# Sums of forms run ahead of their high parts, low parts a step behind, in an FFN's last two up-projections

## The chip, the cores and the metric

The kernel runs on one core of a Trainium2 chip. The metric is the time of one execution in device microseconds (us). A profile of one execution tells what each engine did: TensorE (PE, with PEld for its weight loads), VectorE (DVE), ScalarE (ACT), GpSimd (POOL) and SyncE (SP), which issues most of the loads.

## The reference

A trunk of two layers over 512 frames of width 1024. Each layer has an FFN, a mixer (an mLSTM in the first, a gated MLP in the second), a second FFN and a gated embedding, with a LayerNorm after each. The change touches the four FFNs:

```python
def swiglu_ffn(x, w_gu, w_d):          # w_gu 1024 x 5632, w_d 2816 x 1024
    g, u = jnp.split(x @ w_gu, 2, axis=-1)
    return (jax.nn.silu(g) * u) @ w_d
x = layer_norm(DN_ALPHA * x + 0.5 * swiglu_ffn(x, ffn1_wgu[i], ffn1_wd[i]), ln_g[i, 0], ln_b[i, 0])
```

## The kernel before

**Splitting.** Every float32 operand of a matmul is split in two: a high part, which ScalarE makes by a copy (`whi`, `fhi`), and a low part, the operand less the high part, which VectorE makes by a subtraction (`wlo`, `flo`). A product of two operands is three matmuls (`mm3`, L318 to L320). Some low parts (list `by_dma`, product numbers 1, 2 and 4 of each seven) are made without VectorE: ScalarE writes minus the high part, and GpSimd issues a transfer that adds the operand to it (L243, L244).

**Chunks.** The 2816 hidden columns of an FFN are 22 blocks of 128, worked in six chunks (`FFN_CHUNKS`). The first four chunks are projected up plainly (`fps`). The last two, from `UP_FROM` = 4 on, are projected up by seven products in the place of eight, the Winograd form of Strassen's product, for two blocks (a pair) at a time: `up_products`. So an FFN has four pairs, and 28 products up (`ups`), which the text calls p0 to p27; the number within a pair is r = 0 to 6. The weights of a pair lie in two tiles of 1 MB, `g` and `u`, of two quarters each. Its seven operands are, in order, a11, a12, s2, s1, s3, s4, a22; s1 to s4 are sums, which VectorE makes in place in those quarters (`up_forms`; L139, L140 make s1 and s2, L147 makes s3, L151 makes s4). x's own seven operands are made by `UpForms`: most of them by `steps` during chunk 3, the rest in `last`, at the end of chunk 3.

**Down.** The product down of a chunk (`gps`) is done by seven products too, one after every second product up of the next chunk. Its weights are formed by `forms` (`wquarter`, L110 to L116) and its left operands, the hidden values, by `Group.form` (`h`, `fhi`, `flo`). `Group.add` adds a product to the residual `xt`.

**Order.** The order of instructions on each engine is that in which the code is written; each engine works through its own in order, and waits at an instruction whose operands are not there. In `up_products` a step s issues: the product up; the addition of an earlier product down to `xt`; `pair.take`, which for r = 0, 2 and 3 copies the bank out on ScalarE (L977) and else adds it on VectorE (L980, L985) or multiplies the gate in (L994); `W.release`, which gives the weight's buffer back and so forms and splits the operand four products ahead (`fill`); and, every second step, the product down and the next form of `h`. All r = 0, 2, 4 and 6 of a pair accumulate in one bank, so p(r = 4) can't start before the copy of r = 2, and p(r = 2) not before that of r = 0.

Of the kernel before, what the change touches and what calls it, by code (L numbers as in the profile page):

```python
# [17 lines left out]
P = 128  # L18
# [30 lines left out]
class Weights:  # L49
# [4 lines left out]
    def __init__(self, nc, raw_pool, split_pool):  # L54
# [7 lines left out]
        self.ready, self.taken, self.held = deque(), deque(), []  # L62

# [33 lines left out]
    def forms(self, kind, b11, b12, b22, b21):  # L97
# [23 lines left out]
        for _, make in made:  # L121
            self.in_place.add(make)
        return [(kind, js, make) for js, make in made]

    def up_forms(self, g, u):
# [12 lines left out]
        def s2():  # L138
            vec.tensor_add(quarter(u, 0), quarter(u, 0), quarter(u, 1))  # L139
            vec.tensor_sub(quarter(g, 0), quarter(u, 0), quarter(g, 0))  # L140
            return quarter(g, 0), (g,)

        def s1():
            return quarter(u, 0), ()

        def s3():
            vec.tensor_sub(quarter(u, 0), quarter(u, 1), quarter(g, 0))  # L147
# [65 lines left out]
    def fill(self, most=1000, low=None, meanwhile=None):  # L213

        while most and self.next_split < len(self.order):
# [8 lines left out]
            if js is not None:  # L224
                src, used = make()
                shape = list(src.shape)
# [8 lines left out]
            for i in range(parts):  # L235
# [9 lines left out]
                else:  # L245
# [3 lines left out]
            for j in used:  # L249
                self.left[j] -= 1  # L250
            while self.load():
                pass
        return meanwhile

    def take(self):
# [5 lines left out]
        self.kind, tiles = self.ready.popleft()  # L261
        if not self.kind.startswith("rows"):
            self.taken.append(self.kind)
# [24 lines left out]
def hybrid_trunk(ctx: ExitStack, tc, x, p, ln_g, ln_b, ffn1_wgu, ffn1_wd, ffn2_wgu, ffn2_wd,  # L288
# [540 lines left out]
    class Group:  # L829
# [5 lines left out]
        def __init__(self, h, pool, first=False, by_tokens=False):  # L835
# [4 lines left out]
            self.ready, self.banks = deque(), []  # L840
            self.next_form = self.next_product = self.next_add = 0

        def form(self):

            def a(i, j):
                m = self.half
                if self.by_tokens:
                    return self.h[:, 2 * i - 2:2 * i, (j - 1) * 256:j * 256]
                return self.h[:, m * j - m:m * j, (i - 1) * 256:i * 256]
            a11, a12, a21, a22 = a(1, 1), a(1, 2), a(2, 1), a(2, 2)  # L850
# [4 lines left out]
            if r == 2:  # L855
                vec.tensor_add(a21, a21, a22)
                vec.tensor_sub(a11, a21, a11)  # L857
# [5 lines left out]
            split(hi, lo, (a11, a12, a11, a21, a21, a12, a22)[r])  # L863
            self.ready.append((hi, lo))

        def product(self):
            r = self.next_product
            self.next_product += 1
            w, f = W.take(), self.ready.popleft()
# [21 lines left out]
    class UpForms:  # L891


        def __init__(self, pool, late):
# [36 lines left out]
            def last():  # L931
                split(*self.t3, b)
                d = [tmp_tile("x_d").rearrange("p (k t) -> p k t", k=2) for _ in range(2)]
                for i, s in enumerate(halves):
                    joined(d[i], 1, 0, s)
                    vec.tensor_sub(d[i], d[i], c[:, s])
                vec.tensor_sub(f32r(self.t2, late, "wlo"), c, self.t2[0].bitcast(F32))
                hi, lo = f32r(self.t4, pool, "f1"), f32r(self.t4, pool, "f0")
                for i, s in enumerate(halves):
                    split(hi[:, s], lo[:, s], d[i])  # L940

            self.last = last
# [10 lines left out]
    class UpPair:  # L953
# [19 lines left out]
        def take(self, r):  # L973
# [4 lines left out]
            elif r in (1, 5):  # L978
                g = part[r // 5 * 2]
                vec.tensor_add(g, g, bank[1 if r == 1 else 3])  # L980
                sca.activation(g, g, AF.Silu)
                if r == 5:
                    self.gated(1, g, part[3])
# [4 lines left out]
            if r in (1, 5, 6):  # L988
                up_let_go(self.at[{1: 1, 5: 3, 6: 0}[r]])

# [837 lines left out]
```

## Time and profile before

| | |
|---|---|
| time, median of 3 runs (lowest to highest) | 2350.91 us (2349.48 to 2351.85) |
| the profiled execution | 2349.07 us, its span 2347.4 us |
| PE busy in the span | 2234.5 us (95%) |
| DVE busy | 1716.2 us (73%) |
| ACT busy | 1051.8 us (45%) |
| mean granted clock of TensorE | 0.978 |

A row of a timeline has the start and the length in us, the engine, the line, the operation, out<-in, the shapes, and in brackets the idle time before it and what ended that. A row of windows has a stretch and its length, then the busy time of each engine in it (with the number of instructions), the granted clock of TensorE as a share of full speed, and the share of the transfer engines with their GB/s. A row of waits has engine, line and tile, whom it waited for, us in all, times, and the longest.

### The profile page before, as it was taken

What the parts mean: (1) busy time and instruction counts of PE and PEld (TensorE: products, weight loads), DVE (VectorE), ACT (ScalarE), POOL (GpSimd) and SP (SyncE); (2) the same over time, 40 slices, a digit from 0 to 9 for tenths busy, and PEclk for the clock granted to TensorE, in tenths of its full rate; (3) what the DMA queues carried; (4) which work ended last, traced back from release to release, by engine and by line L of the source; (5) the groups of instructions that cost most, each with busy time, mean ns of one, the idle gap of its engine ahead of it and who ended that gap; (6) DMA issues with size and microseconds to landing.
All of it is one profiled execution on the core that took longest, in us unless ns stands there. A gap on an engine that the chain in (4) does not pass through costs nothing.

```text
span 2347.4 us, 29405 instructions
## 1 busy us (share of the span) xinstructions
PE 2234.5 (95%) x11669; PEld 1922.8 (82%) x11669; DVE 1716.2 (73%) x2468; ACT 1051.8 (45%) x1476; POOL 145.0 (6%) x183
## 2 busy tenths in 40 slices
PE   9999889999999999988899998979999999998898
PEld 8887878888888888877788887878888888887877
DVE  5668677786776676777786768776788767686787
ACT  4334445564646533444444334445345443345442
POOL 1000000111101000000000000000001000000000
PEclk9999889999999999999999999999999999998999
DMA  6324434556846533344433324433438633345341
GB/s 202 111 82 129 117 81 135 126 134 135 163 108 142 153 108 99 108 99 126 126 122 94 124 71 122 126 95 121 142 83 153 170 99 108 99 117 138 87 133 65
DMA packets 213233, 278.91 MB, mean 119 GB/s; under 512 B 6580, under 2 KB 161332, under 8 KB 213096
## 3 DMA queue, kind: packets, MB, share of 16 engines
q1 hardware_dynamic: 168080, 211.83, 27.9%
q0 software_dynamic: 38400, 50.52, 13.8%
q10 hardware_dynamic: 6616, 14.69, 1.8%
q8 instruction: 92, 1.51, 0.3%
q14 instruction: 45, 0.37, 0.1%
HBM read 224.58 MB, written 2.11 MB: 97 GB/s over the span
## 4 chain that ended last, share of the span: by engine, by line
PE 76%; DVE 12%; ACT 6%; issue 4%; DMA 0%; ACTq 0%; POOL 0%; DVEq 0%; POOLq 0%
PE fps L318 8%; PE fps L320 7%; PE fps L319 7%; PE gps L318 5%; PE gps L319 5%; PE gps L320 5%; DVE wlo L246 3%; ACT whi L237 3%; PE ups L318 2%; PE dps L318 2%; PE dps L320 2%; PE dps L319 2%; PE ups L319 2%; PE ups L320 2%; DVE xt L692 2%
## 5 line engine op out<-in xcount | busy, mean ns | idle before, releaser
L237 ACT ACTIVATE whi<-wraw 128x1024 fp32r<-128x1024 f32 (+1 forms) x388 | 400.4, 1048 | 209.1 <-DVE wraw L147 47.9
L246 DVE TENSOR_TENSOR wlo<-wraw,whi 128x1024 fp32r<-128x1024 f32 (+1 forms) x292 | 350.0, 1217 | 81.3 <-ACT whi L237 80.5
L246 DVE TENSOR_TENSOR wlo<-wquarter,whi 128x1024 fp32r<-128x1024 f32 (+1 forms) x140 | 156.3, 1117 | 232.2 <-ACT whi L237 232.2
L318 PE MATMUL fps<-xh,whi 128*128 128x512 f32 x800 | 311.4, 389 | 0.0
L319 PE MATMUL fps<-xl,whi 128*128 128x512 f32 x800 | 311.2, 389 | 0.0
L320 PE MATMUL fps<-xh,wlo 128*128 128x512 f32 x800 | 311.2, 389 | 0.0
L237 ACT ACTIVATE whi<-wquarter 128x1024 fp32r<-128x1024 f32 (+1 forms) x140 | 135.8, 970 | 268.9 <-PE gps L320 103.7
L318 PE MATMUL gps<-whi,fhi 128*128 128x512 f32 x644 | 253.0, 393 | 0.0
L319 PE MATMUL gps<-wlo,fhi 128*128 128x512 f32 x644 | 252.1, 392 | 0.0
L320 PE MATMUL gps<-whi,flo 128*128 128x512 f32 x644 | 251.3, 390 | 0.0
L318 PE MATMUL ups<-xh,whi 128*128 128x256 f32 x512 | 158.9, 310 | 70.4 <-ACT us L977 70.4
L244 POOL DMA_DIRECT2D wlo<-wraw x96 | 100.6, 1048 | 1576.1 <-ACT wlo L243 1493.4
L692 DVE TENSOR_TENSOR xt<-xt,gps 128x512 f32<-128x512 f32 x302 | 193.0, 679 | 0.7 <-PE gps L320 0.7
L320 PEld LDWEIGHTS fps<-xh,wlo 128*128 128x128 f32 x800 | 150.2, 188 | 31.4
L319 PEld LDWEIGHTS fps<-xl,whi 128*128 128x128 f32 x800 | 150.2, 188 | 31.0
L318 PEld LDWEIGHTS fps<-xh,whi 128*128 128x128 f32 x800 | 150.2, 188 | 30.9
L318 PEld LDWEIGHTS ups<-xh,whi 128*128 128x128 f32 x512 | 110.1, 215 | 76.3 <-ACT us L977 75.4
L323 ACT ACTIVATE fhi<-h 128x512 fp32r<-128x512 f32 (+1 forms) x140 | 81.4, 581 | 194.4 <-DVE h L857 53.0
L319 PE MATMUL ups<-xl,whi 128*128 128x256 f32 x512 | 156.1, 305 | 0.0
L320 PE MATMUL ups<-xh,wlo 128*128 128x256 f32 x512 | 155.9, 304 | 0.0
L320 PEld LDWEIGHTS gps<-whi,flo 128*128 128x128 f32 x644 | 121.3, 188 | 26.6
L318 PEld LDWEIGHTS gps<-whi,fhi 128*128 128x128 f32 x644 | 121.8, 189 | 23.9
(357 smaller groups left out, 4964.7 us busy)
## 6 DMA issues: line engine op xcount, KB each, us to landing
wraw<-in_ffn_wgu_dram SPq DMA_DIRECT2D x79, 1024.0 KB, 6.4
wlo<-wraw POOLq DMA_DIRECT2D x96, 512.0 KB, 5.2
wquarter<-in_ffn_wd_dram SPq DMA_DIRECT2D x64, 512.0 KB, 3.8
wraw<-in_ml_w_in_dram SPq DMA_DIRECT2D x24, 1024.0 KB, 5.6
wraw<-in_gm_w_in_dram SPq DMA_DIRECT2D x15, 1024.0 KB, 5.7
wraw<-in_ffn_wgu_dram SPq DMA_DIRECT2D x17, 512.0 KB, 5.0
wraw<-in_ffn_wd_dram SPq DMA_DIRECT2D x8, 1024.0 KB, 4.8
wraw<-in_ml_w_out_dram SPq DMA_DIRECT2D x8, 1024.0 KB, 5.2
```

Source lines behind the costliest of these rows:

```text
L237: self.nc.scalar.activation(hi[:, s], src[:, s], AF.Copy)
L244: self.nc.gpsimd.dma_start(lo[:, s], src[:, s], accum_op=OP.add)
L246: self.nc.vector.tensor_sub(lo[:, s], src[:, s], hi[:, s].bitcast(F32))
L318: mm(ps, st[0], mv[0], start=start, stop=False, skip_group_check=more)
L319: mm(ps, st[0], mv[1], start=False, stop=False, skip_group_check=more)
L320: mm(ps, st[1], mv[0], start=False, stop=stop, skip_group_check=more)
L323: sca.activation(hi, src, AF.Copy)
L692: vec.tensor_add(dst, dst, ps)
```

## The change

In `up_products`, and there alone, three things are apart that were together. `form_ahead` makes the sums of the next three operands in the order as soon as what they overwrite has been split. A low part of VectorE's is not made behind its high part but put on a list, which the next step empties (`lows`, `finish_form`). And x's last operands, made in one go at the end of chunk 3 before, are made at steps 0, 2, 3 and 4 of chunk 4 (`formed.last`). With them: s3 is made in g's first quarter (where s2 was) after s4 in g's second, silu is issued behind the next split (`gate`), and the gate of r = 5 a step later. In `Group`, for all who use it, one subtraction moves from form 5 to form 4, and form 4 has another tile.

ScalarE between the copy of r = 0 and that of r = 3 in the first pair, before. `us` is the value copied out of a bank `ups`; `whi<-wraw` is the high part of an operand up, `whi<-wquarter` that of a weight down. What an instruction waits for stands behind it:

```order
L977 ACTIVATE us_1793<-ups_1768 128x512 [waits PE_49]
L237 ACTIVATE whi_1796<-wraw_1527 128x1024 [waits DVE_49]
L243 ACTIVATE wlo_1797<-wraw_1527 128x1024
L981 ACTIVATE us_1793<-us_1793 128x512 [waits DVE_49]
L237 ACTIVATE whi_1829<-wraw_1470 128x1024 [waits DVE_49,PE_49,Activation_49]
L237 ACTIVATE whi_1851<-wquarter_1145 128x1024 [waits DVE_49,PE_49,Activation_49]
L323 ACTIVATE fhi_1857<-h_1296 128x512 [waits DVE_49,Activation_49]
L977 ACTIVATE us_1887<-ups_1768 128x512 [waits PE_49]
L237 ACTIVATE whi_1889<-wraw_1527 128x1024
L977 ACTIVATE us_1920<-ups_1895 128x512 [waits PE_49,Activation_49]
```

And of the changed kernel:

```order
L1045 ACTIVATE us_1779<-ups_1754 128x512 [waits PE_49]
L358 ACTIVATE xh_87<-x_wlo_1299 128x4x256
L242 ACTIVATE whi_1787<-wraw_1472 128x1024 [waits DVE_49]
L248 ACTIVATE wlo_1788<-wraw_1472 128x1024
L242 ACTIVATE whi_1820<-wraw_1472 128x1024 [waits PE_49,Activation_49]
L1059 ACTIVATE us_1779<-us_1779 128x512 [waits DVE_49]
L242 ACTIVATE whi_1838<-wquarter_1145 128x1024 [waits PE_49,Activation_49]
L905 ACTIVATE fhi_1843<-h_1296 128x512 [waits DVE_49,Activation_49]
L1045 ACTIVATE us_1872<-ups_1754 128x512 [waits PE_49]
L242 ACTIVATE whi_1881<-wraw_1530 128x1024
L1045 ACTIVATE us_1911<-ups_1886 128x512 [waits PE_49]
```

The copies stand where they stood; two of the three high parts between the first two copies no longer wait for VectorE, and x's high part (L358) has come behind the first copy.

VectorE from the sum s2 of the second pair on, before (`wraw` are the quarters up, `wquarter` the weights down):

```order
L139 TENSOR_TENSOR wraw_1833<-wraw_1833 128x1024 [waits DMAHW2_49]
L140 TENSOR_TENSOR wraw_1588<-wraw_1833,wraw_1588 128x1024 [waits DVE_49]
L246 TENSOR_TENSOR wlo_2031<-wquarter_1407,whi_2030 128x1024 [waits Activation_49]
L859 TENSOR_TENSOR h_1296<-h_1296 128x2x256
L324 TENSOR_TENSOR flo_2038<-h_1296,fhi_2037 128x512 [waits PE_49,Activation_49]
L692 TENSOR_TENSOR xt_86<-xt_86,gps_1835 128x512
L692 TENSOR_TENSOR xt_86<-xt_86,gps_1836 128x512
L994 SCALAR_TENSOR_TENSOR h_1767<-us_1793,ups_1768 128x2x256 [waits PE_49]
L246 TENSOR_TENSOR wlo_2069<-wraw_1833,whi_2068 128x1024 [waits Activation_49]
L147 TENSOR_TENSOR wraw_1833<-wraw_1833,wraw_1588 128x1024 [waits DVE_49]
```

And of the changed kernel (DMAHW is a load of SP's, DMASW a transfer of GpSimd's):

```order
L141 TENSOR_TENSOR wraw_1876<-wraw_1876 128x1024 [waits DMAHW2_49,DMASW6_49]
L142 TENSOR_TENSOR wraw_1590<-wraw_1876,wraw_1590 128x1024 [waits DVE_49]
L1048 TENSOR_TENSOR us_1872<-us_1872,ups_1886 128x512 [waits PE_49]
L149 TENSOR_TENSOR wraw_1590<-wraw_1590 128x1024 [waits DMASW7_49,DVE_49,Activation_49]
L150 TENSOR_TENSOR wraw_1590<-wraw_1876,wraw_1590 128x1024 [waits DMASW0_49,DVE_49,Activation_49]
L727 TENSOR_TENSOR xt_86<-xt_86,gps_1824 128x512 [waits PE_49]
L727 TENSOR_TENSOR xt_86<-xt_86,gps_1825 128x512 [waits PE_49]
L1064 SCALAR_TENSOR_TENSOR h_1753<-us_1872,us_1911 128x2x256 [waits Activation_49]
L1064 SCALAR_TENSOR_TENSOR h_1753<-us_1779,ups_1754 128x2x256 [waits PE_49]
L908 TENSOR_TENSOR flo_2037<-h_1296,fhi_2036 128x512 [waits Activation_49]
L257 TENSOR_TENSOR wlo_2034<-wquarter_1409,whi_2033 128x1024
```

s3 (L149, L150; L147 before) has come from the tenth place to the fourth and fifth, and waits for two transfers of GpSimd's, those of a12's and s2's low parts. DMASW7 is the one and DMASW0 the other.

VectorE where x's last operands are made, in the first pair, before (`x_d` and `t_f` are x's fourth sum and its parts, which p6 reads):

```order
L324 TENSOR_TENSOR flo_1748<-h_1296,fhi_1747 128x512 [waits Activation_49]
L324 TENSOR_TENSOR xl_88<-x_wlo_1299,xh_87 128x4x256 [waits Activation_49]
L905 TENSOR_TENSOR x_d_1753<-xh_87,xl_88 128x512
L936 TENSOR_TENSOR x_d_1753<-x_d_1753,x_f0_1300 128x512 [waits DVE_49]
L905 TENSOR_TENSOR x_d_1754<-xh_87,xl_88 128x512
L936 TENSOR_TENSOR x_d_1754<-x_d_1754,x_f0_1300 128x512 [waits DVE_49]
L937 TENSOR_TENSOR t_wlo_1759<-x_f0_1300,t_whi_1651 128x1024
L324 TENSOR_TENSOR t_f0_1762<-x_d_1753,t_f1_1761 128x512 [waits DVE_49,Activation_49]
L324 TENSOR_TENSOR t_f0_1762<-x_d_1754,t_f1_1761 128x512 [waits Activation_49]
L147 TENSOR_TENSOR wraw_1527<-wraw_1527,wraw_1470 128x1024
```

And the end of the same work in the changed kernel, between steps 3 and 4:

```order
L257 TENSOR_TENSOR wlo_1882<-wraw_1530,whi_1881 128x1024 [waits PE_49,Activation_49]
L1002 TENSOR_TENSOR x_d_1302<-x_d_1302,x_f0_1300 128x512
L1002 TENSOR_TENSOR x_d_1303<-x_d_1303,x_f0_1300 128x512
L727 TENSOR_TENSOR xt_86<-xt_86,gps_1924 128x512 [waits PE_49]
L727 TENSOR_TENSOR xt_86<-xt_86,gps_1925 128x512 [waits PE_49]
L1050 TENSOR_TENSOR us_1911<-us_1911,ups_1754 128x512 [waits PE_49,Activation_49]
L908 TENSOR_TENSOR flo_1942<-h_1296,fhi_1941 128x512 [waits Activation_49]
L892 TENSOR_TENSOR h_1296<-h_1296 128x2x256
L893 TENSOR_TENSOR h_1296<-h_1296 128x2x256 [waits DVE_49]
L257 TENSOR_TENSOR wlo_1922<-wraw_1590,whi_1921 128x1024 [waits DMAHW1_49]
L257 TENSOR_TENSOR wlo_1939<-wquarter_1145,whi_1938 128x1024
L1008 TENSOR_TENSOR t_f0_1978<-x_d_1302,t_f1_1917 128x512
```

The low part of x's fourth sum, ahead of all sums and low parts of the pair before, now stands behind those of four steps. The order of TensorE, GpSimd and SP is as it was. The diff, cut to its core:

```diff
@@ up_forms
         def s2():
             vec.tensor_add(quarter(u, 0), quarter(u, 0), quarter(u, 1))
             vec.tensor_sub(quarter(g, 0), quarter(u, 0), quarter(g, 0))
+            return quarter(g, 0), ()
+        def s1():
+            return quarter(u, 0), (u,)
+        def s3():
+            vec.tensor_sub(quarter(g, 1), quarter(g, 1), quarter(g, 0))
+            vec.tensor_sub(quarter(g, 0), quarter(u, 1), quarter(g, 0))
             return quarter(g, 0), (g,)
-        def s1():
-            return quarter(u, 0), ()
-        def s3():
-            vec.tensor_sub(quarter(u, 0), quarter(u, 1), quarter(g, 0))
-            return quarter(u, 0), (u,)
         def s4():
-            vec.tensor_sub(quarter(g, 1), quarter(g, 1), quarter(g, 0))
             return quarter(g, 1), (g,)
...
+        self.after.update({s2: (a11,), s3: (a12, s2)})
@@ fill
-                src, used = make()
+                while any(m not in self.formed for m in self.after.get(make, ())):
+                    self.lows(1)
+                src, used = self.made.pop(make, None) or make()
...
-                else:
+                elif not self.apart:
                     self.nc.vector.tensor_sub(lo[:, s], src[:, s], hi[:, s].bitcast(F32))
...
-            for j in used:
-                self.left[j] -= 1
-            while self.load():
-                pass
+            def done(make=make, used=used, src=src, hi=hi, lo=lo, late=self.apart and make not in self.by_dma):
+                if late:
+                    self.nc.vector.tensor_sub(lo, src, hi.bitcast(F32))
+                self.formed.add(make)
+                for j in used:
+                    self.left[j] -= 1
+                while self.load():
+                    pass
+            if self.apart and make not in self.by_dma:
+                self.pending.append((lo, done))
+            else:
+                done()
+    def lows(self, most=100):
+        for _ in range(min(most, len(self.pending))):
+            self.pending.popleft()[1]()
+    def form_ahead(self, n):
+        for kind, js, make in self.order[self.next_split:self.next_split + n]:
+            if js is None or make in self.made or make not in self.in_place:
+                continue
+            if any(m not in self.formed for m in self.after.get(make, ())):
+                continue
...
+            self.made[make] = make()
@@ Group
+        def sums(self, r):
...
+            elif r == 4:
+                vec.tensor_sub(a12, a12, a11)
+                vec.tensor_sub(a11, a22, a11)
...
-            elif r == 4:
-                vec.tensor_sub(a21, a22, a11)
-            elif r == 5:
-                vec.tensor_sub(a12, a12, a11)
...
+            def low():
+                vec.tensor_sub(lo, src, hi.bitcast(F32))
+                self.low = None
+                if r in (1, 3) and apart:
+                    self.sums(r + 1)
+                    self.summed.add(r + 1)
@@ UpForms
-            def last():
-                split(*self.t3, b)
-                d = [tmp_tile("x_d").rearrange("p (k t) -> p k t", k=2) for _ in range(2)]
...
+            d = [tmp.tile([P, 2, 256], F32, name="x_d", tag="pad", bufs=3) for _ in range(2)]
...
+            self.last = {0: t3_t2, 2: x21, 3: t4, 4: t4_low}
@@ up_products, step s
+                    if r == 6:
+                        pair.gated(1, pair.part[2], pair.part[3])
                     pair.take(r)
+                    group.finish_form()
+                    W.lows()
+                    if c == UP_FROM and s in formed.last:
+                        formed.last[s]()
                     W.release()
+                    pair.gate(r)
+                    W.form_ahead(3)
                     if s % 2:
                         group.product()
                         W.release(kind="rows")
-                        group.form()
+                        group.form(True)
```

More of the change, by code (lines that the diff above doesn't have):

```diff
@@ L122, in forms @@
             self.in_place.add(make)
+        self.after.update({t2: (made[0][1],), t1: (made[1][1], t2)})
         return [(kind, js, make) for js, make in made]
@@ L840, in __init__, with part, form @@
             self.ready, self.banks = deque(), []
+            self.low, self.summed = None, set()
             self.next_form = self.next_product = self.next_add = 0
[L843 to L850, printed above, removed]
+        def part(self, i, j):
+            m = self.half
+            if self.by_tokens:
+                return self.h[:, 2 * i - 2:2 * i, (j - 1) * 256:j * 256]
+            return self.h[:, m * j - m:m * j, (i - 1) * 256:i * 256]
+        def sums(self, r):
+            a11, a12, a21, a22 = self.part(1, 1), self.part(1, 2), self.part(2, 1), self.part(2, 2)
+            if r == 2:
+                vec.tensor_add(a21, a21, a22)
+                vec.tensor_sub(a11, a21, a11)
+            elif r == 4:
+                vec.tensor_sub(a12, a12, a11)
+                vec.tensor_sub(a11, a22, a11)
+        def form(self, apart=False):
             r = self.next_form
@@ L989, in take, with gate @@
                 up_let_go(self.at[{1: 1, 5: 3, 6: 0}[r]])
+        def gate(self, r):
+            if r in (1, 5):
+                g = self.part[r // 5 * 2]
+                sca.activation(g, g, AF.Silu)
         def gated(self, t, g, u):
```

43 lines of the change are left out of this document (31 added, 12 removed).

## The prediction

> **What bounds the kernel now.** I read the page first, then the waits and the lines of the first stage of products (p0 to p27 of the first FFN), then the timelines of ScalarE and VectorE around its first stall.
>
> ```profile
> span 2347.4 us, 29405 instructions
> PE 2234.5 (95%) x11669; PEld 1922.8 (82%) x11669; DVE 1716.2 (73%) x2468; ACT 1051.8 (45%) x1476; POOL 145.0 (6%) x183
> ...
> L318 PE MATMUL ups<-xh,whi 128*128 128x256 f32 x512 | 158.9, 310 | 70.4 <-ACT us L977 70.4
> ```
>
> TensorE is the bound, and most of its 113 us of idle time stands ahead of the products of the changed chunks, released by ScalarE's copies out of the bank (L977). The four stages, by windows (width, then busy us of PE, PEld, DVE, ACT, POOL, granted clock, DMA):
>
> ```profile
> 212.98:363.10 150.12, 128.22 (x830) 119.72 (x829) 110.39 (x129) 70.94 (x89) 8.41 (x10) 0.91 0.42 110
> 1000.26:1150.20 149.94, 126.05 (x838) 117.14 (x837) 109.49 (x130) 70.53 (x89) 8.48 (x10) 0.92 0.43 113
> 1441.64:1591.80 150.16, 126.40 (x830) 117.76 (x829) 110.39 (x129) 70.97 (x89) 8.51 (x10) 0.93 0.42 111
> 2100.92:2252.00 151.08, 128.66 (x838) 119.99 (x837) 109.49 (x130) 70.53 (x89) 8.48 (x10) 0.91 0.42 112
> ```
>
> They are alike, so I work out one and take it four times. Each loses 21.9 us (150.1 less 128.2) to idle PE and runs at a mean clock of 0.91 to 0.93. In the first one:
>
> ```profile
> PE ups L318 <- ACT us L977: 21.9, 6, 5.9
> ...
> 231.80 1.06 ACT L237 ACTIVATE whi<-wquarter 128x1024 fp32r<-128x1024 f32 x1 [3.77 <-DVE wquarter L111]
> 235.53 0.63 ACT L323 ACTIVATE fhi<-h 128x512 fp32r<-128x512 f32 x1 [2.68 <-DVE h L857]
> 236.07 0.58 ACT L977 ACTIVATE us<-ups 128x512 f32<-128x512 f32 x1
> ...
> 236.70 0.58 PE L318 MATMUL ups<-xh,whi 128*128 128x256 f32 x1 [5.93 <-ACT us L977]
> ...
> 247.66 0.34 PE L318 MATMUL ups<-t_f,whi 128*128 128x256 f32 x1
> ...
> 273.50 0.58 PE L318 MATMUL ups<-xh,whi 128*128 128x256 f32 x1 [5.69 <-ACT us L977]
> ...
> 311.51 0.58 PE L318 MATMUL ups<-xh,whi 128*128 128x256 f32 x1 [3.94 <-ACT us L977]
> ...
> 338.47 0.58 PE L318 MATMUL ups<-t_whi,whi 128*128 128x256 f32 x1 [4.35 <-ACT us L977]
> ...
> 351.44 0.39 PE L318 MATMUL ups<-xh,whi 128*128 128x256 f32 x1 [1.59 <-ACT us L977]
> ```
>
> The PE rows are p4, p6, p11, p18, p23 and p25. ScalarE works in order. The copy that p4 needs stands behind two high parts whose sums VectorE had not made yet; VectorE in turn waits for high parts before it makes low parts. That is the chain that the change cuts. Without waits a product up takes 2.88 us and one down 2.75:
>
> ```profile
> 284.83 0.28 PE L318 MATMUL ups<-t_f,whi 128*128 128x256 f32 x1
> ...
> 287.71 0.40 PE L318 MATMUL gps<-whi,fhi 128*128 128x512 f32 x1
> ...
> 290.46 0.28 PE L318 MATMUL ups<-xh,whi 128*128 128x256 f32 x1
> ```
>
> 28 up and the 13 down between them are 116.6 us with the last one's drain, against 150.1. The stalls also cost clock:
>
> ```profile
> 236.70:242.19 5.49, 5.49 (x26) 5.49 (x27) 5.46 (x7) 2.33 (x3) 0.00 (x0) 0.51 0.32 96
> 241.99:245.07 3.08, 3.08 (x26) 3.08 (x26) 1.89 (x2) 2.23 (x3) 0.00 (x0) 0.99 0.57 196
> ...
> 1578.61:1582.91 4.30, 4.30 (x25) 4.30 (x26) 4.09 (x5) 3.79 (x5) 0.00 (x0) 0.67 0.56 187
> ```
>
> p4, after a stall of 5.93, took 5.49 us at clock 0.51; p5 took 3.08 at 0.99. So a long stall costs some 2.6 us more behind it.
>
> **The change, part by part.** No instruction is added: DVE keeps its 110 us a stage, which fit into 116.6 only if it hardly waits. I follow DVE's new order with these steps from start to start: a whole tile (128x1024) 1.14, or 1.25 where the next one reads it; a half (128x512) 0.60, or 0.72.
>
> ```profile
> 214.10 1.23 DVE L246 TENSOR_TENSOR wlo<-wraw,whi 128x1024 fp32r<-128x1024 f32 x1 [0.23 <-ACT whi L237]
> 215.24 1.22 DVE L246 TENSOR_TENSOR wlo<-wquarter,whi 128x1024 fp32r<-128x1024 f32 x1
> 216.38 0.68 DVE L324 TENSOR_TENSOR flo<-h,fhi 128x512 fp32r<-128x512 f32 x1
> 216.98 1.22 DVE L324 TENSOR_TENSOR xl<-x_wlo,xh 128x1024 fp32r<-128x1024 f32 x1
> ...
> 218.11 0.68 DVE L905 TENSOR_TENSOR x_d<-xh,xl 128x512 f32<-128x512 f32 x1
> 218.83 0.69 DVE L936 TENSOR_TENSOR x_d<-x_d,x_f 128x512 f32<-128x512 f32 x1
> ...
> 229.21 1.22 DVE L110 TENSOR_TENSOR wquarter<-wquarter 128x1024 f32<-128x1024 f32 x1
> 230.46 1.23 DVE L111 TENSOR_TENSOR wquarter<-wquarter 128x1024 f32<-128x1024 f32 x1
> ```
>
> *Sums ahead, low parts a step behind (pair 0).* The copy for p4 now waits only for ScalarE's own queue: xl's low part starts at 217.6, as ScalarE ends its high part (p0's end 216.0, the first copy 0.6, the high part 1.0); five whole steps (1.14, 1.14, 1.25, 1.14, 1.25) and its own 1.2 bring L112, the row's sum, to its end at 224.8, an add and the sums L889 and L890 (0.6, 0.72, 0.69) end at 226.7, and on ScalarE a high part and the copy (0.6 each, 0.2 between) end at 228.1. PE can reach p4 at 212.98 + 4 x 2.88 + 2 x 2.75 = 230.0. The stall of 5.93 goes.
>
> *x's sums spread.* What is late next is p6, which needs the low part of x's fourth sum (L1008). From DVE's first instruction of the stage (213.2) up to its first half there stand 15 whole and 19 half steps: 17.4 + 11.8 = 29.2 us, and 1.8 of waits for ScalarE, so it ends at about 244.8. PE would reach p6 at 238.5: a stall of 6.2 us, and 2.6 of clock. Before, the same work stood ahead of p2 and was paid in p4's stall. So the spreading by itself moves this stall by two products; p6 starts 2.9 us earlier than its 247.7 of before.
>
> *The third sum now in g's first quarter (a new wait).* s3 (L149, L150) overwrites what the transfers of a12's and s2's low parts read, and in pairs 1 to 3 it stands right behind s2. DVE therefore waits until s2's transfer has landed:
>
> ```profile
> 224.55 1.06 ACT L237 ACTIVATE whi<-wraw 128x1024 fp32r<-128x1024 f32 x1 [2.55 <-DVE wraw L147]
> 225.52 1.04 ACT L243 ACTIVATE wlo<-wraw 128x1024 fp32r<-128x1024 f32 x1
> 226.85 0.83 POOL L244 DMA_DIRECT2D wlo<-wraw  x1 [16.93 <-ACT wlo L243]
> ...
> DMA to landing us min/median/max: 4.5/4.9/5.1
> ```
>
> From s2's sum: two ACT instructions 2.0, 0.3 to POOL, 4.9 to land, 7.3 us in all, of which DVE fills 1.9 with the us add and L149. No row shows DVE in this wait, so I bound it: 0 if the transfer is early, 5.4 if DVE comes at once. I take the counted value for each pair.
>
> Pair 1: s2's sum ends at 247.8, the transfer lands at 255.1, L150 ends at 256.4. Behind it are queued two adds to xt, two gates, the down form's low part and row 4's low part: 4.2 us, 260.5. PE comes to that product down at 244.8 + 4 x 2.88 + 2.75 + 2.6 = 261.7. No stall, with 1.2 us to spare; without the half clock ahead of it, 1.4.
>
> Pair 2: PE reaches the end of p12 at 275.8, where s2's high part gets its buffer; landing 283.2, L150 ends at 284.4, and what waits for it (the next group's first form) is due at 287. No stall.
>
> Pair 3: from 284.4 DVE has 13 whole and 18 half steps up to s2's sum, 26.2 us without a pause: 310.7. ACT 2.0, POOL 0.3, landing 318.0, L150 to 319.3. Then come the adds (1.2), the two gates and two splits of the last chunk in turn with ACT (3.6), and on ACT one high part before the copy that frees p23's bank: 325.5. PE comes to p23 at 318.0. Stall 7.5, clock 2.6. Before, p23 stalled too, by 4.4, and p11, p18 and p25 by 5.7, 3.9 and 1.6; those three are gone, since no copy stands behind a sum there.
>
> *Other edits.* Silu after the next split, and the second gate a step later: 0.6 us of ACT or DVE each, ahead of nothing that PE awaits within 2 products; 0. The form's subtraction moved from its sixth to its fifth form in all other stages: 0.6 us, covered by PE's own work, as in the stretch just before:
>
> ```profile
> 200.00:213.00 13.00, 13.00 (x59) 10.74 (x59) 10.93 (x15) 5.92 (x8) 0.85 (x1) 1.00 0.45 92
> ...
> wraw<-in_ffn_wgu_dram SPq DMA_DIRECT2D x5, 1024.0 KB, 5.5
> ```
>
> If that cover were gone it would cost 0.6 for each of 25 forms, 15 us. The loads of u and g are issued a step later, once low parts are done: at 230 for pair 1, landing 5.5 later, 10 us ahead of need.
>
> **Sum.** p23 at 325.5, then 5 x 2.88 + 2 x 2.75 + 2.6 of clock and 0.2: p27 ends at 348.2 instead of 363.1, 14.9 us less; four stages 60. The profiled execution took 2349.1 (its span and 1.7 around it), so 2289; the median of the runs stands 1.8 above it: 2291.
>
> The Trainium skill ("DMA: Bandwidth & Descriptors", Anatomy of one DMA) fits a transfer issued by GpSimd with 2.0 us plus its bytes by 436 GB/s, an estimate of 3.2 us for these 512 KB. The trace has 4.9, and by 3.2 pairs 2 and 3 would each shed 1.7, giving 2277; the trace's figure is used.
>
> **Rivals.**
> A, better: pair 3's copy comes in time, because DVE runs ahead of my count there; then only p6's stall is left: 116.6 + 6.2 + 2.6 = 125.4 a stage, 99 us less, 2252. For it: PE has 7.5 us to lose in one place only. Against it: DVE has 26 us of work in one piece before it.
> B, slower: DVE's wait for the transfer. Each us of landing beyond 4.9 delays pairs 2 and 3 in full and pair 1 nearly, 2.5 us a stage; from 10.9 us on the gain is gone. If it stands behind a12's transfer and a weight load (4.9 + 4.9 + 5.5 = 15.3), a stage takes 11 us more than before, 2395. Against it: no transfer of POOL's took over 5.1 here, and a12's is issued some 8 us ahead.
> C, the change doesn't do what it says: DVE, busy for 110 of 150 us, swaps its waits for high parts for waits for transfers and x's low part, and stalls move but don't shrink: 2351.
> The Trainium skill ("TensorE: Matmul & The Clock Gate", HAM oscillation) has gaps over some 3.4 us bring the half clock back. The row at 1578.61 shows a clock of 0.67 after a stall of 2.75 already, so I don't count on short stalls being free.
>
> **Chances.** The forecast 0.60 (its own range 2265 to 2325, landing 4.5 to 7 us and a stall more or less), A 0.20, B 0.10, C 0.10. A measurement of this kernel can tell about 0.2%. Faster by more: 0.60 + 0.20 + 0.02 of C; within: 0.06 of C; slower: B and 0.02 of C. The range runs from below A to the forecast's end, 2245 to 2330, and leaves C and B out.
>
> **What the profile after would show.** p4, p11, p18 and p25 without a stall; p6 waiting some 6 us for L1008; p23 some 7 for the copy L1045; DVE idle ahead of L150 three times a stage until a transfer lands; two half-clock stretches a stage instead of four; stages of 135 us with DVE's 110 unchanged. I would be wrong if L150's wait reaches PE in pairs 1 and 2 (too high a gain), or if DVE is ahead by p23 (too low).

## The result, and the profile after

The changed kernel takes 2287.05 us (median of 4 runs, 2286.30 to 2289.04), the kernel before 2350.62 beside it (2349.48 to 2351.85): a ratio of 0.9731, 95% interval 0.9714 to 0.9748. The forecast was 2291.

The page of the changed kernel, its first lines and the group of the products up that read x's fourth sum:

```profile
span 2285.1 us, 29387 instructions
PE 2214.1 (97%) x11669; PEld 1908.1 (84%) x11669; DVE 1711.5 (75%) x2468; ACT 1049.7 (46%) x1476; POOL 145.4 (6%) x183
...
L354 PE MATMUL ups<-t_f,whi 128*128 128x256 f32 x128 | 40.8, 319 | 23.1 <-DVE t_f L1008 23.1
```

The span less PE's busy time is 71.0 us, where it was 112.9. The rest of the 62 us that the span lost is PE's own busy time, 20.4 us less for the same instructions; the mean granted clock rose from 0.978 to 0.985. The four stages of products up, as windows (width, then busy us of PE, PEld, DVE, ACT, POOL, granted clock, DMA):

```profile
213.27:346.22 132.95, 120.25 (x830) 113.09 (x829) 108.75 (x129) 70.28 (x89) 8.41 (x10) 0.95 0.47 123
983.57:1118.26 134.69, 121.83 (x838) 114.63 (x837) 107.99 (x130) 69.95 (x89) 8.50 (x10) 0.95 0.47 126
1409.61:1543.67 134.06, 121.48 (x830) 114.35 (x829) 108.99 (x129) 70.52 (x89) 8.53 (x10) 0.95 0.47 122
2052.58:2189.09 136.51, 122.48 (x838) 115.00 (x837) 108.00 (x130) 69.81 (x89) 8.50 (x10) 0.94 0.46 124
```

Against 150.12, 149.94, 150.16 and 151.08 they are 17.2, 15.3, 16.1 and 14.6 us shorter, 63.1 together: all of the gain. DVE is busy nearly as long as before (108.8 us in the first stage, where it was 110.4). Whom PE and then DVE waited for in the first stage (in all, times, longest), and the PE rows of p4, p6, p11, p18, p23 and p25:

```profile
PE ups L353 <- ACT us L1045: 6.7, 1, 6.7
PE ups L354 <- DVE t_f L1008: 5.8, 1, 5.8
...
DVE wraw L150 <- DMA wlo<-wraw: 13.6, 3, 5.3
...
230.23 0.28 PE L353 MATMUL ups<-xh,whi 128*128 128x256 f32 x1
...
239.08 0.35 PE L353 MATMUL ups<-t_f,whi 128*128 128x256 f32 x1 [0.18 <-DVE us L1050]
245.20 0.58 PE L354 MATMUL ups<-t_f,whi 128*128 128x256 f32 x1 [5.77 <-DVE t_f L1008]
...
266.86 0.28 PE L353 MATMUL ups<-xh,whi 128*128 128x256 f32 x1
...
297.94 0.28 PE L353 MATMUL ups<-xh,whi 128*128 128x256 f32 x1
...
324.72 0.58 PE L353 MATMUL ups<-t_whi,whi 128*128 128x256 f32 x1 [6.75 <-ACT us L1045]
...
334.69 0.28 PE L353 MATMUL ups<-xh,whi 128*128 128x256 f32 x1
```

p4, p11, p18 and p25 start without a wait. Two stalls are left: p6, which did not wait before and now waits for x's low part at the end of DVE's backlog, and p23, which waits for a copy, 6.75 us in the place of 4.35. DVE's timeline shows where p23's wait comes from:

```profile
255.17 1.23 DVE L150 TENSOR_TENSOR wraw<-wraw 128x1024 f32<-128x1024 f32 x1 [5.30 <-DMA wlo<-wraw]
...
273.56 1.23 DVE L141 TENSOR_TENSOR wraw<-wraw 128x1024 f32<-128x1024 f32 x1 [1.42 <-DMA wraw<-in_ffn_wgu_dram]
...
283.10 1.23 DVE L150 TENSOR_TENSOR wraw<-wraw 128x1024 f32<-128x1024 f32 x1 [2.99 <-DMA wlo<-wraw]
...
317.56 1.23 DVE L150 TENSOR_TENSOR wraw<-wraw 128x1024 f32<-128x1024 f32 x1 [5.32 <-DMA wlo<-wraw]
...
319.90 0.69 DVE L1064 SCALAR_TENSOR_TENSOR us<-us 128x512 f32<-128x512 f32 x1
321.28 0.69 DVE L359 TENSOR_TENSOR wquarter<-us,wquarter 128x512 fp32r<-128x512 f32 x1 [0.70 <-ACT wquarter L358]
```

In all three pairs DVE stands at L150, the second half of s3, until the transfer of s2's low part has landed. In pairs 1 and 2 PE does not feel it. In pair 3 the last chunk's gates and splits stand behind it, and behind those, on ScalarE, the copy for p23.

### The profile page after: what moved, and what is told of

It is laid out like the page before. It is cut to its first block, busy times and chain, and to the rows that moved or that the text cites. A ratio compares the mean times of both kernels' runs of the same rounds, so it can differ in the third digit from the quotient of the medians.

```text
span 2285.1 us, 29387 instructions
## 1 busy us (share of the span) xinstructions
PE 2214.1 (97%) x11669; PEld 1908.1 (84%) x11669; DVE 1711.5 (75%) x2468; ACT 1049.7 (46%) x1476; POOL 145.4 (6%) x183
## 4 chain that ended last, share of the span: by engine, by line
PE 84%; DVE 9%; ACT 2%; DMA 2%; issue 2%; DVEq 0%; ACTq 0%; POOL 0%; POOLq 0%
PE fps L353 8%; PE fps L355 8%; PE fps L354 8%; PE gps L355 6%; PE gps L353 6%; PE gps L354 6%; DVE wlo L257 3%; PE ups L354 2%; PE ups L353 2%; PE ups L355 2%; PE dps L354 2%; PE dps L353 2%; PE dps L355 2%; DMA wlo<-wraw 2%; PE gups L353 1%
## 5 line engine op out<-in xcount | busy, mean ns | idle before, releaser
L353 PE MATMUL fps<-xh,whi 128*128 128x512 f32 x800 | 311.4, 389 | 0.0
L251 DVE TENSOR_TENSOR wlo<-wraw,whi 128x1024 fp32r<-128x1024 f32 (+1 forms) x210 | 252.4, 1217 | 48.0 <-ACT whi L242 47.2
L353 PE MATMUL gps<-whi,fhi 128*128 128x512 f32 x644 | 251.9, 391 | 0.0
L251 DVE TENSOR_TENSOR wlo<-wquarter,whi 128x1024 fp32r<-128x1024 f32 (+1 forms) x92 | 97.7, 1062 | 160.8 <-ACT whi L242 160.8
L353 PEld LDWEIGHTS fps<-xh,whi 128*128 128x128 f32 x800 | 150.2, 188 | 31.1
L353 PE MATMUL ups<-xh,whi 128*128 128x256 f32 x512 | 145.2, 284 | 0.0
L354 PE MATMUL ups<-xl,whi 128*128 128x256 f32 x512 | 145.0, 283 | 0.0
L355 PE MATMUL ups<-xh,wlo 128*128 128x256 f32 x512 | 145.0, 283 | 0.0
L353 PEld LDWEIGHTS gps<-whi,fhi 128*128 128x128 f32 x644 | 121.2, 188 | 23.9
L354 PEld LDWEIGHTS gps<-wlo,fhi 128*128 128x128 f32 x644 | 121.1, 188 | 23.7
```

What stands on the lines that cost most here:

```text
L251: self.nc.vector.tensor_sub(lo[:, s], src[:, s], hi[:, s].bitcast(F32))
L353: mm(ps, st[0], mv[0], start=start, stop=False, skip_group_check=more)
L354: mm(ps, st[0], mv[1], start=False, stop=False, skip_group_check=more)
L355: mm(ps, st[1], mv[0], start=False, stop=stop, skip_group_check=more)
```

## The experiments

All kernels were timed against the kernel before. Those called "the changed kernel" with something undone or added differ from it only there.

| | us, median | ratio to before, 95% interval |
|---|---|---|
| the changed kernel | 2287.05 | 0.9731 (0.9714 to 0.9748) |
| x's last sums at once | 2280.67 | 0.9697 (0.9683 to 0.9712) |
| no sums ahead | 2258.61 | 0.9607 (0.9593 to 0.9621) |
| low parts at once | 2294.70 | 0.9759 (0.9745 to 0.9774) |
| neither sums ahead nor late low parts | 2349.25 | 0.9997 (0.9987 to 1.0006) |
| no sums ahead, x at once | 2250.22 | 0.9574 (0.9558 to 0.9590) |
| sums two ahead | 2253.48 | 0.9583 (0.9567 to 0.9599) |
| s3 in u | 2256.02 | 0.9600 (0.9585 to 0.9614) |
| two ahead, x's low part first | 2238.95 | 0.9526 (0.9512 to 0.9540) |
| no sums ahead, x's low part first | 2251.36 | 0.9579 (0.9566 to 0.9592) |
| two ahead, x at once | 2235.97 | 0.9515 (0.9502 to 0.9528) |
| two ahead, x a step earlier | 2235.88 | 0.9515 (0.9502 to 0.9528) |
| the same, x's copies behind p5's | 2237.27 | 0.9518 (0.9505 to 0.9531) |

### Which part of the change brings the gain

**No sums ahead.** My theory was that the copies came free because the sums were ahead of their high parts.

```diff
-                if r in (1, 3) and apart:
+                if False:
...
-                    W.form_ahead(3)
+                    W.form_ahead(0)
```

> The changed kernel without sums ahead: neither the sums of the next operands up nor those of the hidden values are made ahead of their step; low parts still follow a step behind, and x's sums stay spread. Theory (copies stood behind high parts that waited for sums): high parts of ScalarE's wait for sums again and the copies behind them too, so stalls of 3 to 6 us come back at p4, p11 and p18 with their half clock: 2320 to 2345 us. Rival (it was the late low parts that let DVE run ahead): those stalls stay away, 2300 us or less.

Measured: 2258.61 us, 28 less than the changed kernel. The theory fell and the rival held: p4, p11 and p18 do not wait. In the first stage p6's stall is 3.05 us and p23's 0.87; p25 waits twice, 1.34 and 0.87. ScalarE's queue ahead of the copy for p4 in this kernel:

```profile
222.13 1.06 ACT L242 ACTIVATE whi<-wraw 128x1024 fp32r<-128x1024 f32 x1 [4.95 <-DVE wraw L150]
...
224.04 1.04 ACT L242 ACTIVATE whi<-wraw 128x1024 fp32r<-128x1024 f32 x1
...
225.51 1.04 ACT L242 ACTIVATE whi<-wquarter 128x1024 fp32r<-128x1024 f32 x1
226.51 0.64 ACT L905 ACTIVATE fhi<-h 128x512 fp32r<-128x512 f32 x1
227.05 0.58 ACT L1045 ACTIVATE us<-ups 128x512 f32<-128x512 f32 x1
```

The copy still stands behind high parts of weights and of hidden values whose sums DVE makes just ahead of them, and it comes at 227.05 in the place of 236.07. DVE, in its own timeline, stops for ScalarE only twice between 213 and 227, for 0.8 us in all, so the sums are there. Standing behind a sum costs nothing where the sum is early.

**Low parts at once.** The other half undone: sums ahead, but each low part directly behind its high part.

```diff
-                elif not self.apart:
+                else:
                     self.nc.vector.tensor_sub(lo[:, s], src[:, s], hi[:, s].bitcast(F32))
...
-            if self.apart and make not in self.by_dma:
-                self.pending.append((lo, done))
-            else:
-                done()
+            done()
...
-            if not apart:
-                low()
+            low()
```

> The changed kernel with each low part of VectorE's directly behind its high part again, up and down, and the sums still ahead. Theory: DVE waits for ScalarE's high part ahead of each of them (1 to 3.8 us, as the trace of before shows), 20 or so times a stage, and has no slack for it in the second half of a pair: 2300 to 2325 us. Rival (sums ahead are all that matters): 2287 us, the same.

Measured: 2294.70 us, 8 more than the changed kernel, and outside both forecasts. What DVE and PE waited for in its first stage (L350 is the changed kernel's L353, and L1046 its L1050, the add of r = 4; L251 makes the low parts):

```profile
DVE wlo L251 <- ACT whi L242: 12.8, 13, 2.1
DVE wraw L150 <- DMA wlo<-wraw: 7.4, 3, 4.4
...
248.87 0.55 PE L350 MATMUL ups<-t_f,whi 128*128 128x256 f32 x1 [8.84 <-DVE us L1046]
...
315.51 0.58 PE L350 MATMUL ups<-t_f,whi 128*128 128x256 f32 x1 [4.59 <-DVE us L1046]
```

DVE waits for high parts again, but less than half as long as the kernel with neither part does (29.2 us, below), and it waits less for s2's transfer: 7.4 us in the place of 13.6. p6 now waits 8.8 for an add behind DVE's backlog, p20 4.6, and p23 no longer stalls.

**Neither.** So with either half undone most of the gain stays, or more than all of it. Without both, only x's spread sums, s3's other place and the order of silu and the gates are left of the change.

> The changed kernel without sums ahead and with each low part directly behind its high part; x's sums stay spread, s3 in g's first quarter. Each of the two undone alone took no more than 8 us from the gain, or added to it (2258.6 and 2294.7). Theory now (the two do the same thing: DVE's wait for a high part and ScalarE's wait for a sum feed each other, and taking away either one lets DVE reach the sums before the copies are due): with neither, the stalls at p4, p11 and p18 are back, 2320 to 2350 us. Rival (neither counts; x's spread sums or the other order of s3 and silu took the copies' waits away): 2300 us or less.

Measured: 2349.25 us, 0.9997 of the kernel before (0.9987 to 1.0006): all of the gain is gone. In its first stage PE, then DVE, waited for:

```profile
PE ups L350 <- ACT us L1041: 17.2, 5, 4.8
PE ups L350 <- DVE us L1046: 5.8, 2, 5.1
...
DVE wlo L251 <- ACT whi L242: 29.2, 17, 3.6
```

p4, p11, p18, p23 and p25 wait for copies again, and p6 waits 5.1 us for an add. DVE's wait for high parts of weights in the first stage of the kernel before, and of the changed one:

```profile
DVE wlo L246 <- ACT whi L237: 27.4, 18, 3.1
...
DVE wlo L251 <- ACT whi L242: 0.2, 1, 0.2
```

The four kernels together show it: the gain is that DVE and ScalarE no longer wait for each other in turn, DVE for a high part and ScalarE for the next sum. That loop is cut by taking either wait out of it. With sums three ahead, taking out both adds nothing to late low parts alone; with sums two ahead it adds some, as the later runs show. What sums ahead alone are worth with the wait for s2's transfer taken away too was not run.

**x's sums at once.** The spreading undone, the rest kept:

```diff
-                    if c == UP_FROM and s in formed.last:
-                        formed.last[s]()
...
                     while formed.steps:
                         formed.step()
+                    for last in formed.last.values():
+                        last()
```

> The changed kernel, with x's last sums made in one go at the end of chunk 3 again, as before the change. Theory (the gain comes from ScalarE's copies no longer standing behind sums; DVE's chain of work is the bound): p6's stall of 5.95 us and its half clock (2.6) go, a smaller stall comes back at p4 (2 to 3 us, since DVE starts the stage with the same sums ahead of it), and what is saved is mostly given back at the product down of row 4, for which DVE is not ready before 260.5 us whatever PE does: 2280 to 2290 us, within 0.3% of the changed kernel's 2287. Rival (spreading x's sums is what took p4's stall away): p4's stall of 5.9 us and its half clock come back in all four stages and p6's goes only in part, 2300 us or more; if all of the gain is the spreading's, 2340.

Measured: 2280.67 us, as the theory had it. PE in its first stage, at p2, the product down ahead of p10, and p23:

```profile
223.52 0.39 PE L353 MATMUL ups<-t_whi,whi 128*128 128x256 f32 x1 [1.42 <-ACT us L1045]
...
258.87 0.50 PE L354 MATMUL gps<-wlo,fhi 128*128 128x512 f32 x1 [2.37 <-DVE wlo L257]
...
323.76 0.58 PE L353 MATMUL ups<-t_whi,whi 128*128 128x256 f32 x1 [8.30 <-ACT us L1045]
```

p6's stall is gone, 1.4 us come back (at p2; p4 waits 0.5), and in this stage all that was saved is lost again behind L150's wait: 2.4 us at the product down, and p23's stall grows from 6.75 to 8.30. In the third and the fourth stage p23's stall does not grow (6.5 us in both, where it was 6.6 and 8.1). The spreading was worth nothing here: it cost 6 us.

**No sums ahead, x at once.** Both of the last edits in one kernel, so that the late low parts and s3's place are all that is left.

> The changed kernel without sums ahead and with x's last sums in one go at the end of chunk 3; of the change, late low parts and s3's place are left. Theory (the late low parts alone are enough, and x's sums only move a stall between p4 and p6): p6's stall of 3.05 us goes, one of 1 to 4 us comes at p2 or p4, 2250 to 2275 us beside 2258.6. Rival (spread sums are needed where no sum runs ahead): p4's stall of 5.9 us and its half clock come back, 2280 us or more.

Measured: 2250.22 us, at the fast edge of the theory's range. The late low parts alone do it, and bring 100 us; with x at once it is 8 us faster than with x spread. In the first stage p2 waits 1.42; p25 waits twice, 1.34 and 0.88, and no other product over 0.9.

### The two stalls that are left

**Sums two ahead.** s3 is the third operand ahead; two ahead, it is made a step later, behind the gates.

```diff
-                    W.form_ahead(3)
+                    W.form_ahead(2)
```

> The changed kernel with sums made two operands ahead in the place of three. Only s3 moves by it: it comes one step later, behind the gates and splits that the copy ahead of p23 stands behind. Theory (p23's stall of 6.6 to 8.1 us is s3's wait for s2's transfer, 5.3 us, and s3 itself, 2.2, ahead of those gates): p23's stall and its half clock (1.5) go, 8.2 us a stage, 2254 us. Rival (the stall is the gates' and splits' own, 3.6 us, or the wait comes back a step later ahead of another product): 2280 to 2290 us.

Measured: 2253.48 us, 0.5 from the theory's figure. Of DVE's three waits at L150 one is left in the stage, in pair 2 and of 0.8 us. p23 starts on time, and p6 is PE's only stall:

```profile
PE ups L354 <- DVE t_f L1008: 5.8, 1, 5.8
...
DVE wraw L150 <- DMA wlo<-wraw: 0.8, 1, 0.8
```

**s3 in u.** The same stall, taken away in another way: s3 stays ahead of the gates but is made where it need not wait.

```diff
         def s3():
-            vec.tensor_sub(quarter(g, 1), quarter(g, 1), quarter(g, 0))
-            vec.tensor_sub(quarter(g, 0), quarter(u, 1), quarter(g, 0))
-            return quarter(g, 0), (g,)
+            vec.tensor_sub(quarter(u, 0), quarter(u, 1), quarter(g, 0))
+            return quarter(u, 0), (u,)
         def s4():
+            vec.tensor_sub(quarter(g, 1), quarter(g, 1), quarter(g, 0))
             return quarter(g, 1), (g,)
...
-        self.after.update({s2: (a11,), s3: (a12, s2)})
+        self.after.update({s2: (a11,), s3: (s1,), s4: (a12, s2)})
```

> The changed kernel with s3 made in u's first quarter again (s1's place, as before the change), so that it waits for no transfer, but still three operands ahead, so it stays ahead of the gates and splits as it is now (s4's subtraction moves from s3 to s4). Theory (p23's stall is the wait of 5.3 us for s2's transfer): DVE comes 5.3 us earlier to the gates, 1.4 to 2 us of stall are left, without half clock: about 4 x 6.8 us less than 2287, 2260 us. Rival (s3's own sums ahead of the gates are what counts): one whole sum of 1.25 us less stands there, so 4 x 1.25 us, 2282 us; no gain if u's buffer, held longer now, makes the next load late.

Measured: 2256.02 us, 31 less. p23's stall is gone here too, and p6's is as it was. The two kernels together show that p23's stall was the wait for the transfer and not the place of the sum: with the wait gone, a sum ahead of the gates did next to no harm.

**Two ahead, and x's low part first.** L1008 ahead of the low parts and sums of step 4:

```diff
                     pair.take(r)
+                    if c == UP_FROM and s == 4:
+                        formed.last[4]()
                     group.finish_form()
                     W.lows()
-                    if c == UP_FROM and s in formed.last:
+                    if c == UP_FROM and s in (0, 2, 3):
                         formed.last[s]()
                     W.release()
                     pair.gate(r)
-                    W.form_ahead(3)
+                    W.form_ahead(2)
```

> Two edits in the changed kernel: sums two operands ahead (2253.5 us by itself), and the low part of x's fourth sum (L1008) ahead of the low parts and sums that stand in front of it at step 4. Theory (p6 waits for DVE's backlog): L1008 starts right behind the add of r = 4, at about 238.5 us in the place of 244.0, p6's stall and its half clock go in all four stages, 8.4 us each: 2220 us (2215 to 2235). Rival (the lack is only passed on, to the product down of row 4 whose low part now comes later): 2240 to 2253 us.

Measured: 2238.95 us, between the two forecasts and on the rival's edge. p6's stall went (5.95 to 0.3 us), but the stage became only 3.5 us shorter than with two ahead alone. In its first stage PE waited for:

```profile
PE ups L355 <- DMA wlo<-wraw: 1.7, 2, 0.9
PE ups L353 <- ACT us L1045: 0.8, 2, 0.6
PE ups L355 <- DVE wlo L257: 0.6, 1, 0.6
```

These stand in p7, p9 and p25. p7's is for a low part that L1008 has overtaken. To p9 and p25 PE comes earlier than with two ahead alone, by 6.4 and 4.3 us from the stage's start, but the transfers that they read land only 1.2 and 3.5 us earlier. So more than half of the 8.4 us is lost again in other waits.

**No sums ahead, and x's low part first.** Are sums ahead worth anything, once p6 is out of the way?

> The changed kernel without sums ahead (2258.6 us by itself) and with L1008 first at step 4. Theory: p6's stall of 3.05 us and its half clock (1.7) go, 4.7 us a stage; the short stalls of p23 and p25 (0.9, 1.3 and 0.9 us) stay, since their sums are made just when ScalarE needs them: 2240 us. That would be the price of no sums ahead at all beside two ahead (2239): none. Rival (sums ahead are worth what they were meant for, some us a stage): 2250 us or more.

Measured: 2251.36 us against 2238.95 with sums two ahead: the rival's. Short waits stay at p9, p11, p23 and p25 (2.7 us for copies, 2.5 for transfers in the first stage), which fits sums made only just in time, though no run shows that by itself. So sums two ahead are worth 12 us here, and 5 us beside the kernel without sums ahead in which p6's stall stays (2253.48 against 2258.61); the third one ahead costs 34.

**Two ahead, x at once.**

> The changed kernel with sums two operands ahead and x's last sums in one go at the end of chunk 3: both of the stalls left are taken on, p23's by the later s3, p6's by the earlier x. Theory (x's sums fit ahead of p0 as well as anywhere, once low parts are late; the spreading only moved them to a place where DVE has no slack): of the 2280.7 us with x at once, p23's stall (8.3), its half clock (2.5) and the product down's wait of 2.4 go, 13 us a stage: 2230 us (2225 to 2238). Rival (the lack of DVE's time is passed on, to p2 and p4): 2240 us or more.

Measured: 2235.97 us, the theory's, near the slow end of its range; beside the kernel without sums ahead and with x at once (2250.22) sums two ahead are worth 14 us. The first stage has no half clock and is 120.95 us long:

```profile
213.10:334.05 120.95, 117.71 (x830) 110.05 (x829) 109.04 (x129) 69.87 (x89) 8.41 (x10) 1.00 0.51 135
```

**Two ahead, x a step earlier.**

```diff
-            self.last = {0: t3_t2, 2: x21, 3: t4, 4: t4_low}
+            self.last = {0: t3_t2, 1: x21, 2: t4, 3: t4_low}
```

> The changed kernel with sums two operands ahead and x's last operands made at steps 0, 1, 2 and 3 in the place of 0, 2, 3 and 4. Theory (p6 waits for the place that L1008 has in DVE's order): one step earlier, L1008 stands ahead of some 6 us of other work, p6's stall of 5.8 us and its half clock go: 2222 to 2235 us. Rival (the work ahead of p7 stays the same, so the lack is passed on to the low parts that p7 and the next product down read): 2239 to 2250 us, as with L1008 put first at step 4 (2239).

Measured: 2235.88 us, 0.9 above the theory's range and 3 below the rival's. p6 no longer waits, but p5 does: PE's row, and ScalarE's queue ahead of the copy of r = 3.

```profile
235.30 0.58 PE L353 MATMUL ups<-xh,whi 128*128 128x256 f32 x1 [2.48 <-ACT us L1045]
...
232.58 1.24 ACT L1003 ACTIVATE t_f<-x_d 128x512 fp32r<-128x512 f32 x2 [3.49 <-DVE x_d L1002]
...
234.67 0.58 ACT L1045 ACTIVATE us<-ups 128x512 f32<-128x512 f32 x1
```

It is the old pattern: a copy that frees a bank behind a high part (L1003) whose sum comes late.

**The same, x's copies behind p5's.** L1003 is moved from step 2 into step 3:

```diff
                     vec.tensor_sub(d[i], d[i], c[:, s])
+
+            def t4_parts():
+                for i, s in enumerate(halves):
                     sca.activation(f32r(self.t4, pool, "f1")[:, s] if not i else self.t4[0][:, s], d[i], AF.Copy)
...
             def t4_low():
+                t4_parts()
                 lo = f32r(self.t4, pool, "f0")
```

> The kernel of the run before with x's last operands a step earlier (2235.9 us), with one edit: the two copies that make the high part of x's fourth sum (L1003) are issued at step 3, behind the copy of r = 3, and no longer at step 2 ahead of it. In that run p5 waited 2.48 us for this copy, and half clock followed: p5 and p6 began 5.5 and 7.0 us after the products before them, in the place of 2.9 and 5.6. Theory (a copy that frees a bank must not stand behind a high part whose sum DVE has still to make): p5's stall and its clock go, 4 us a stage, 2220 us (2216 to 2226). Rival (DVE's backlog is passed on to p6 or p7): 2232 us or more.

Measured: 2237.27 us, the rival's: no gain. The copy comes in time, p5 does not wait, and p6 waits 1.38 us for DVE's add of r = 4 instead, p9 1.3 for a copy and a transfer. A window of the first 37 us of its stage, up into p8, fits that forecast:

```profile
213.26:250.26 37.00, 35.62 (x254) 33.32 (x253) 34.88 (x42) 20.26 (x26) 2.50 (x3) 1.00 0.37 100
```

DVE is busy for 34.9 of 37 us, PE for 35.6, so little of either is left to gain there. Four kernels with four places for x's sums lie between 2236 and 2239, each with its wait at another product. Two ahead with x at once or a step earlier is the best found: 4.9% less than the kernel before, and 51 us less than the changed one.

## Why the prediction was right, and what in it was not

- **The copies' stalls.** p4, p11, p18 and p25 without a wait: right in all four stages. The cause was named as one chain, and that is shown: with neither part the gain is gone. But the working took sums ahead as what frees the copies ("no copy stands behind a sum there"), and they are not needed for it: without them the copies come in time too, and the kernel is 28 us faster.
- **p6.** Forecast start 244.8 after 6.2 us of stall; measured 245.20 after 5.95 in two pieces. The count of steps on DVE, from start to start, was right to 0.4 us over 32 us. DVE's waits on the way were 2.1 us, where 1.8 were put. "The spreading by itself moves this stall" is borne out: undone, p6's stall is gone and p2 waits, and the kernel is 6 us faster.
- **DVE's wait at L150.** Forecast at 5.4 us where DVE comes at once; measured 5.30 in pair 1 and 5.32 in pair 3, and 2.99 in pair 2, for which no wait was worked out. Ends of L150 forecast at 256.4, 284.4 and 319.3; measured 256.4, 284.3 and 318.8. In pair 1 the end is right to 0.1 us by luck: GpSimd began the transfer at 250.56, 0.5 later than counted, and L150 started 4.6 us after that, where 4.9 was put for the landing alone. Rival B's 10.9 was far off.

```profile
250.56 0.83 POOL L249 DMA_DIRECT2D wlo<-wraw  x1 [7.31 <-ACT wlo L248]
```

- **The load of g and u.** "10 us ahead of need" is right for pair 1, of which it was said: issued at 230.13, and L141 starts at 245.66. It does not hold for pair 2: there the load was issued at 266.36, as the late low part that SyncE waited for ended, and DVE waited 1.42 us for it at L141, up to 273.56. It took some 7 us, where 5.5 was put; the load beside it (269.34) took 7.0 too. L150 waited for the transfer behind it anyway, and no product was late.
- **p23.** Forecast 325.5 after 7.5 us, measured 324.72 after 6.75. PE's own arrival, put at 318.0, is 318.4 by the prediction's steps (10 x 2.88 and 5 x 2.75 behind 275.8); PE came at 317.97. The half clock behind it was put at 2.6 and cost 1.5: p23 took 4.53 us, at a mean clock of 0.65, and a product at full clock takes 3.0 with its drain.

```profile
324.72:329.25 4.53, 4.53 (x25) 4.53 (x26) 4.53 (x7) 4.53 (x6) 0.85 (x1) 0.65 0.23 45
```

- **The sum.** 14.9 us a stage were forecast, 17.2, 15.3, 16.1 and 14.6 measured. The first stage's 2.3 us too little are the 0.8 by which p23 started early, the 1.1 of clock behind it, and 0.3 by which the stage began later. The 21.9 us of idle PE, given for each stage before, are the first one's; the others' rows give 23.9, 23.8 and 22.4, in stages of nearly the same length. Times four it was 60 against 63.6, so 2291 against 2287.
- **Rival A**, a kernel with only p6's stall left, was priced at 2252. It did not come about, but the kernel with sums two ahead is that case: 2253.5.
- **The transfer's price.** The estimate of 3.2 us by the Trainium skill ("DMA: Bandwidth & Descriptors", Anatomy of one DMA) does not agree with this case: the same 4.6 us from GpSimd's issue to L150's start stand against it.

## What to carry to other kernels

Where two in-order engines feed each other, each waiting for the other's last result, look for the loop and cut it at one place; the second cut may bring little, and the work that it moves early can take the place of work that is due. Before an operation is moved ahead, list what its operands wait for: a sum three operands ahead, which had to wait 5.3 us for a transfer, cost 34 us; two ahead, p25, which reads it, waited 1.4 us in one stage of four and next to nothing in the others. And when moving a late piece only moves the wait, look at the busy share of its engine in that stretch, not in the stage: at 94% over 37 us, order had little left to give here.

## What the runs showed of the hardware

Half clock came in pieces of 3.4 us: one, two, or three in a row (10.2 us from 319.65 on, with x at once). Four windows in a row around p6's stall in the changed kernel (width, PE busy, granted clock):

```profile
239.20:242.60 3.40, 0.23 (x1) 1.00 0.34 114
242.60:246.00 3.40, 0.80 (x3) 0.50 0.71 135
246.00:249.40 3.40, 3.40 (x17) 0.50 0.63 181
249.40:252.80 3.40, 3.40 (x31) 1.00 0.30 58
```

PE went idle at 239.4; the clock halves 3.2 us later, within the stall, and stays so for two such pieces. So what a stall costs depends on how much of the half clock falls into the stall itself: p6's 5.77 us hid 2.6 us of it and p23's 6.75 hid 3.6, and p23 paid 1.5 us behind its stall, where p4, after 5.93, paid 2.6 before. And a stall shorter than a piece can bring one on: p5's 2.48 us in the kernel with x a step earlier, here in its first and then in its second stage.

```profile
231.50:234.90 3.40, 1.32 (x12) 0.99 0.87 280
234.90:238.30 3.40, 3.00 (x14) 0.50 0.20 48
...
991.80:995.20 3.40, 0.92 (x8) 1.00 0.77 266
995.20:998.60 3.40, 3.40 (x25) 1.00 0.50 155
```

The Trainium skill ("TensorE: Matmul & The Clock Gate", HAM oscillation) gives idle times over some 3.4 us as the mark; by these rows 2.48 us were enough in the first stage and the same 2.48 us were not in the second, so the length of a wait alone does not decide it. p2's 1.42 us in the kernel with two ahead and x at once brought no half clock.
